# Expert stream of a mixture-of-experts stage: one copy and one split traced elsewhere, rows of empty slots left out of the gather

## The chip, the cores and the metric

One core of a Trainium2 chip runs the whole kernel. The time is device microseconds (us) of one execution; lower is better. The kernel before was run three times, and one more execution was profiled.

## The reference, cut to what matters

The network has two halves. The first (attention and a gated delta rule, two layers) is untouched. The second has two layers, and each ends in a mixture of experts over 512 tokens of width 1024:

```python
def hier_moe(x, ...):                       # 512 tokens, 32 experts, 2 experts a token
    pg_top, g_top = lax.top_k(softmax(xf @ w_rg + b_rg), 1)      # one of 4 groups
    top_p, top_i = lax.top_k(softmax(le_sel), 2)                 # two experts of its 8
    ...
    def expert_block(args):
        idx, e = args
        xb = x_pad[idx]                                          # rows of the tokens routed to e
        hb = jax.nn.silu(xb @ w_gate[e]) * (xb @ w_up[e])        # 1024 -> 512, twice
        return hb @ w_down[e]                                    # 512 -> 1024
```

Every token has two experts, so 1024 (token, expert) pairs are to be computed in each layer. All 32 experts' weights are read in float32: 2 MB each for gate, up and down.

## The kernel before, in words

**Slots.** The kernel gives every expert 64 slots (`BLK`), 2048 in a layer; `route` (L1336) finds for each slot the pair that sits in it, or none. It leaves two integer tables: `tk`, the token of each slot, one column for a pair of experts (L1425 to L1429), and `mp`, the row of the result that each slot is written to (L1430). `tokens` (L1483) makes the first from the matmul result `mps` in two VectorE instructions; an empty slot has 0 there and is given token 0. `slots` (L1489) makes the second, also in two; an empty slot is given an index far above the bound. An expert with more than 64 pairs would be finished in a loop on the device (`For_i`, L1661), whose count is read by every engine.

**Gather.** `rows` (L1496) writes the normalised tokens to a table `xr` in HBM, 512 rows of 4 KB, in four transfers from POOL's queue (L1507). `gather` (L1517) fetches the 128 rows of two experts' slots with one indirect DMA on POOL's queue (L1522) into a tile `xg` of 128x1024, of which there are two in turn. In its second part (after the `yield`) TensorE transposes the tile into two PSUM tiles (L1532), and each half is split into a high part `pk` (ScalarE, L425) and a low part (VectorE, L426; `split`, L412). The last quarter of the second half is also copied whole into `xf` (ScalarE, L1538), after that half's split. Both the split's VectorE part and the copy read the same PSUM tile. Indices over the bound are left out by the indirect DMA (`oob_is_err=False`); the scatter of the results (`finish`, L1616, DMA at L1624) already uses this.

**Expert stream.** `experts` (L1727) walks over units: eight for an expert's gate and up weights, then three for the down weights of the expert before. For the unit six places ahead (`AHEAD`) it cuts the weights into a high and a low part (`cut`, L1565: ScalarE L425, then VectorE L426), then it does the matmuls of the present unit (`inner` L1576, `outer` L1604). Weights come in tiles of 1 MB through SP's queue (L1561), six per expert, into six buffers. `middle` (L1586) stands between gate/up and down: 16 small TensorE products, a tanh on ScalarE (L1596), two VectorE instructions (L1597, L1598), and a split of the result into `hk` (ScalarE L425, VectorE L426). It is traced behind unit (e, 0, 1), and its result is used by the down matmuls behind unit (e, 3, 1). A copy of a finished accumulator to `tmp` (ScalarE, L1765) frees it for the next one.

**Order.** TensorE, VectorE and ScalarE keep the traced order: `pin` (L1627) chains each engine's instructions of the stream. POOL's and SP's instructions are not chained; the scheduler orders them by priority and readiness. Each engine works through its own instructions in order, so one that waits holds up all that stand behind it.

**Before the stream.** `moe` (L1643) routes, gathers the first pair, computes the overflow count (`further`), asks for the first weights and passes the loop, which ran no iteration here. The following pairs are gathered inside `experts`, one for every two experts, 16 in a layer.

Of the kernel before, what the change touches and what calls it, by code (L numbers as in the profile page):

```python
# [13 lines left out]
I32 = mybir.dt.int32  # L14
# [3 lines left out]
OP = mybir.AluOpType  # L18
AX = mybir.AxisListType

P = 128
D = 1024
# [12 lines left out]
N_EXP, D_EXP = 32, 512  # L35
BLK = 64
# [143 lines left out]
class Net:  # L180
# [1155 lines left out]
    def route(self, i):  # L1336

        nc, a = self.nc, self.a
        v, act, pe = nc.vector, nc.scalar, nc.tensor
        X, rstd, gx = self.x_in  # L1340
        ps = self.acc()[:72]
# [11 lines left out]
        table = self.rows(i, gx, rstd)  # L1353
# [36 lines left out]
        for c in range(NC):  # L1390
            o = rk[:, 32 * c:32 * c + 32]
# [3 lines left out]
        for c in range(NC):  # L1395
# [4 lines left out]
                               op0=OP.add, op1=OP.mult)  # L1400
# [16 lines left out]
        mps = self.aux()[:, 0:32]  # L1417
        for k in range(2):
# [3 lines left out]
            for c in range(NC):  # L1422
                pe.matmul(mps, R[:, c].rearrange("p b s -> p (b s)"), idk[:, k, c], start=(k + c == 0),
                          stop=(k == 1 and c == NC - 1))
        tk = self.t([P, N_EXP // 2], "tk", 1, I32)  # L1425
        tk2 = self.t([P, N_EXP], "tk2", 1, I32)
        self.tokens(tk2, mps)
        for b in range(2):
            v.tensor_copy(tk[b * BLK:(b + 1) * BLK], tk2[b * BLK:(b + 1) * BLK, b::2])  # L1429
        mp = self.t([BLK, N_EXP], "mp", 1, I32)  # L1430
        self.slots(mp, mps[:BLK])

        def weights():

# [22 lines left out]
        def further():  # L1457
# [20 lines left out]
            v.tensor_copy(more[:, 0:1], nst[:, 31:32])  # L1478
            v.tensor_scalar(more[:, 1:], bx, float(N_EXP - 1), None, op0=OP.min)
            return place, more  # L1480
        return table, tk, mp, further, weights

    def tokens(self, tk, ps):  # L1483

        v = self.nc.vector
        v.tensor_scalar(tk, ps, -1.0, 0.0, op0=OP.add, op1=OP.max)
        v.tensor_scalar(tk, tk, 1, None, op0=OP.logical_shift_right)

    def slots(self, mp, ps):  # L1489

        v = self.nc.vector
        em = self.t([BLK, N_EXP], "em", 1)[:, :ps.shape[1]]
        v.tensor_scalar(em, ps, 0.0, float(1 << 20), op0=OP.is_equal, op1=OP.mult)
        v.scalar_tensor_tensor(mp, ps, -1.0, em, op0=OP.add, op1=OP.add)

# [18 lines left out]
            self.nc.tensor.transpose(tp[:, j * P:(j + 1) * P], x(j)[:, c * P:(c + 1) * P], self.ident)  # L1514
        return tp

    def gather(self, table, idx, m):  # L1517

        nc = self.nc
        v, act, pe = nc.vector, nc.scalar, nc.tensor  # L1520
        xg = self.t([P, D], "xg", 2)
        nc.gpsimd.indirect_dma_start(out=xg[:m], out_offset=None, in_=table[:, :],  # L1522
                                     in_offset=bass.IndirectOffsetOnAxis(ap=idx, axis=0),
                                     bounds_check=S - 1, oob_is_err=False)
        yield
        n = m // BLK
        pk = self.t([P, KT, n, P], "pk", 2, FR)
        xf = self.t([P, n, BLK], "xf", 2)
        for half in range(2):
            tp = self.aux()  # L1530
            for k in range(4):
                pe.transpose(tp[:, k * m:(k + 1) * m], xg[:m, (4 * half + k) * P:(4 * half + k + 1) * P],  # L1532
                             self.ident[:m, :m])
            tv = tp[:, 0:4 * m].rearrange("p (k e t) -> p k e t", k=4, e=n)
            o = pk[:, 4 * half:4 * half + 4]
            self.split(o[:, :, :, 0:BLK], o[:, :, :, BLK:P], tv)
            if half:
                act.activation(xf, tv[:, 3], AF.Copy)  # L1538
        yield [(pk[:, :, e], xf[:, e]) for e in range(n)]

    def apart(self, ins, first):
# [44 lines left out]
    def middle(self, gu):  # L1586

        nc = self.nc
        v, act, pe = nc.vector, nc.scalar, nc.tensor
        fp = self.aux()  # L1590
        for q in range(2):
            for f in range(4):
                pe.matmul(fp[:, (4 * q + f) * BLK:(4 * q + f + 1) * BLK], gu[q][:, f * P:(f + 1) * P], self.fold,  # L1593
                          start=True, stop=True)
        th = self.t([P, 4 * BLK], "mth", 2)
        act.activation(th, fp[:, 0:256], AF.Tanh, scale=0.5)  # L1596
        v.scalar_tensor_tensor(th, th, 1.0, fp[:, 0:256], op0=OP.add, op1=OP.mult)  # L1597
        v.scalar_tensor_tensor(th, th, 0.5, fp[:, 256:512], op0=OP.mult, op1=OP.mult)  # L1598
        hk = self.t([P, 4, P], "hk", 2, FR)
        hv = th.rearrange("p (f t) -> p f t", f=4)  # L1600
        self.split(hk[:, :, 0:BLK], hk[:, :, BLK:P], hv)
        return hk, hv

    def outer(self, pss, hid, k, h, l, also):  # L1604

# [37 lines left out]
    def moe(self, i, xs, nxt):  # L1643
        nc, a = self.nc, self.a
        v, act, pe = nc.vector, nc.scalar, nc.tensor
        self.compute = [nc.tensor.engine, nc.vector.engine, nc.scalar.engine]
        ym = self.dram.tile([N_SLOT, D], F32, name=f"ym{i}", tag=f"ym{i}", bufs=1)
        table, tk, mp, further, weights = self.route(i)
        pair = lambda q: self.gather(table, tk[:, q:q + 1], P)
        g = pair(0)  # L1650
        next(g)
        place, more = further()

        ws = {}
        for k in range(2):
            ws[0, k] = self.weights(i, 0, k)
        cb = self.t([P, 1], "cb", 1)
        v.memset(cb, 0.0)
        with self.tc.issue_after(self.load.ins):
            extra = nc.values_load(more[0:1, 0:1], min_val=0, max_val=MAX_OVF)  # L1660
        with self.tc.For_i(0, extra, 1) as b:  # L1661
            eo = nc.sync.value_load(more[0:1, bass.ds(b + 1, 1)], min_val=0, max_val=N_EXP - 1)
            sl = self.t([P, BLK], "sl", 1)
            v.tensor_scalar(sl, self.slot1, cb, None, op0=OP.add)
            v.tensor_scalar(cb, cb, float(BLK), None, op0=OP.add)
            bc = lambda x: x.unsqueeze(1).to_broadcast([P, NC, BLK])
            mps = self.aux()[:BLK, 0:1]
            for k in range(2):
                sk = self.t([P, S], "bc", 3).rearrange("p (c s) -> p c s", c=2 * NC)[:, 0:NC]
                v.tensor_tensor(sk, place[:, k * NC:(k + 1) * NC].unsqueeze(2).to_broadcast([P, NC, BLK]), bc(sl),  # L1670
                                op=OP.is_equal)
                for c in range(NC):
                    pe.matmul(mps, sk[:, c], self.ids[:, k * NC + c:k * NC + c + 1], start=(k + c == 0),
                              stop=(k == 1 and c == NC - 1))
            mc, tc = self.t([BLK, 1], "mc", 1, I32), self.t([BLK, 1], "tc", 1, I32)
            self.slots(mc, mps)
            self.tokens(tc, mps)
            go = self.gather(table, tc, BLK)
            next(go)
            self.overflow(i, eo, next(go)[0], mc, ym)  # L1680
        self.tc.no_sync_barrier()
        wt = self.experts(i, ws, [next(g)], pair, mp, ym, weights)
        self.plan((a["w_ple_gate_2"][i], D, 0, D))
        self.fetch(1)
        pp = self.ple_products(i)

        for g in range(2):
            mg = [self.t([P, 2, 2, S], "X", 4) for _ in range(2)]
            for c in range(NC):
                yc = mg[c // 2][:, c % 2]  # L1690
                nc.sync.dma_start(yc, ym.rearrange("(c p k) d -> c p k d", p=P, k=2)[c][:, :, g * S:(g + 1) * S])
                act.activation(yc[:, 0], yc[:, 0], AF.Copy, scale=wt[:, 0, c:c + 1])
                v.scalar_tensor_tensor(yc[:, 0], yc[:, 1], wt[:, 1, c:c + 1], yc[:, 0], op0=OP.mult, op1=OP.add)
            for j in range(4):
                tp = self.transpose4(lambda c: mg[c // 2][:, c % 2, 0, j * P:(j + 1) * P])
                v.tensor_add(xs[4 * g + j], xs[4 * g + j], tp)
                nxt.add(4 * g + j, xs[4 * g + j])
        return pp

    def overflow(self, i, e, x, mp, ym):  # L1700

        room = lambda: self.t([P, S], "bc", 3)
        gu = []
        for up in range(2):
            ps = self.acc()
            for k in range(0, KT, 2):
                w = self.weights(i, e, 2 * up + k // 4, k // 2 % 2)
                m = 1 if k == KT - 2 else 2
# [1 line left out]
                self.inner(ps, x, k, h[:, :m], l[:, :m], w[:, 1] if m == 1 else None)  # L1710
            gu.append(room())
            self.nc.scalar.activation(gu[up], ps, AF.Copy)
        hid = self.middle(gu)
        pss = [self.acc() for _ in range(2)]

        for k in (0, 1):
# [10 lines left out]
    def experts(self, i, ws, xs2, pair, mp, ym, weights):  # L1727
# [3 lines left out]
        nc = self.nc  # L1731
# [8 lines left out]
        acc, gu, hid, g = {}, {}, {}, None  # L1740
        self.pinned = [None, None, {}]
        for n in range(len(units) + AHEAD):
            if n < len(units):
                e, k, part = units[n]
# [3 lines left out]
                m = 1 if k in (1, 3) and part else 2  # L1748
# [6 lines left out]
            e, k, part = units[n - AHEAD]  # L1755
            if k < 4:
# [7 lines left out]
                    gu.setdefault(e, []).append(self.tmp())  # L1764
                    act.activation(gu[e][-1], acc[e], AF.Copy)  # L1765
                if (k, part) == (0, 1) and e:
                    hid[e - 1] = self.middle(gu.pop(e - 1))
                if (k, part) == (2, 1) and e % 2 and e + 1 < N_EXP:
                    xs2.append(next(g))
                if (e, k, part) == (2, 2, 0):  # L1770
# [1 line left out]
            else:  # L1772
                r = k % 2 * 2 + part
                if e == N_EXP - 1 and r == 0:
                    hid[e] = self.middle(gu.pop(e))
                if r == 0:
                    acc[e, "y"] = [self.acc() for _ in range(2)]
                self.outer(acc[e, "y"], hid[e], r, *ready.popleft())
# [179 lines left out]
```

## Time and profile before

| | |
|---|---|
| median of 3 runs | 3080.62 us (3080.24 to 3084.62) |
| profiled execution | 3084.05 us, span 3082.3 us |
| TensorE clock granted over the span | 0.975 |
| busy: TensorE, VectorE, ScalarE, POOL | 93%, 80%, 57%, 15% |
| bytes moved by DMA | 599.29 MB, 248663 packets |
| first expert stream | about 1586 to 2112 us |
| second expert stream | about 2444 to 2968 us |

How to read it: the profile's page gives busy times of the engines over the span, a strip of 40 slices of 77 us, the DMA queues with their bytes, and groups of instructions by line. Other views of the same execution, used below, give busy times and DMA rates of chosen stretches, what each engine waited for, instructions in order of time, and the chain of waits that ended last. Engines: PE is TensorE's matmul, PEld its weight load, DVE VectorE, ACT ScalarE, POOL GpSimd, SPq SyncE's queue. The end of a matmul is modelled, so the start of the next one says more. Shares of busy time are averages over stages with different limits.

### The profile page before, as it was taken

What the parts mean: (1) busy time and instruction counts of PE and PEld (TensorE: products, weight loads), DVE (VectorE), ACT (ScalarE), POOL (GpSimd) and SP (SyncE); (2) the same over time, 40 slices, a digit from 0 to 9 for tenths busy, and PEclk for the clock granted to TensorE, in tenths of its full rate; (3) what the DMA queues carried; (4) which work ended last, traced back from release to release, by engine and by line L of the source; (5) the groups of instructions that cost most, each with busy time, mean ns of one, the idle gap of its engine ahead of it and who ended that gap; (6) DMA issues with size and microseconds to landing.
All of it is one profiled execution on the core that took longest, in us unless ns stands there. A gap on an engine that the chain in (4) does not pass through costs nothing.

```text
span 3082.3 us, 39081 instructions
## 1 busy us (share of the span) xinstructions
PE 2881.6 (93%) x13517; PEld 2160.2 (70%) x13517; DVE 2464.3 (80%) x4540; ACT 1756.1 (57%) x2953; POOL 472.8 (15%) x457
## 2 busy tenths in 40 slices
PE   7998999999999999999979999998998799999987
PEld 6677778886787778878856666665776566666656
DVE  7899787867999578855558888887789588888876
ACT  3454343544454433542357877776476577777874
POOL 1111110011121010120011121111122111121112
PEclk9999999999999999999989999999999899999998
DMA  5211122242222222241259999997123399999981
GB/s 156 82 62 62 62 77 69 83 128 94 74 62 61 77 69 79 86 130 62 95 216 396 406 404 401 407 399 277 65 86 110 151 385 405 404 408 408 406 313 59
DMA packets 248663, 599.29 MB, mean 194 GB/s; under 512 B 29212, under 2 KB 159726, under 8 KB 215694
## 3 DMA queue, kind: packets, MB, share of 16 engines
q1 hardware_dynamic: 237582, 567.38, 49.1%
q0 software_dynamic: 10880, 29.37, 2.7%
q8 instruction: 108, 1.77, 0.2%
q14 instruction: 93, 0.76, 0.1%
HBM read 573.60 MB, written 31.49 MB: 196 GB/s over the span
## 4 chain that ended last, share of the span: by engine, by line
PE 38%; issue 33%; DVE 18%; POOL 7%; ACT 3%; DMA 2%; POOLq 0%; SPq 0%; ACTq 0%; DVEq 0%
PE acc L522 9%; PE acc L521 9%; PE acc L520 9%; POOL ym L1624 4%; DVE wl L426 3%; DVE tmp L953 2%; PE aux L432 1%; POOL xg L1522 1%; PE aux L463 1%; PE aux L843 1%; DMA xg<-xr,tk 1%; PE aux L1111 1%; PE aux L1106 1%; DVE r L1082 1%; DVE r L1081 1%
## 5 line engine op out<-in xcount | busy, mean ns | idle before, releaser
L425 ACT ACTIVATE wh<-w 128x1024 fp32r<-128x1024 f32 (+1 forms) x592 | 577.8, 1003 | 370.2 <-PE acc L521 323.0
L426 DVE TENSOR_TENSOR wl<-w,wh 128x1024 fp32r<-128x1024 f32 (+1 forms) x592 | 674.1, 1164 | 71.1 <-ACT wh L425 66.7
L520 PE MATMUL acc<-X,wh 128*128 128x512 f32 (+1 forms) x1504 | 606.3, 403 | 18.5 <-DVE tmp L898 6.4
L521 PE MATMUL acc<-X,wh 128*128 128x512 f32 (+1 forms) x1536 | 615.8, 401 | 0.6 <-DVE X L426 0.6
L522 PE MATMUL acc<-X,wl 128*128 128x512 f32 (+1 forms) x1504 | 601.9, 401 | 4.9 <-DVE wl L426 4.9
L426 DVE TENSOR_TENSOR X<-w,X 128x1024 fp32r<-128x1024 f32 (+1 forms) x352 | 380.9, 1122 | 64.0 <-ACT X L425 63.2
L425 ACT ACTIVATE X<-w 128x1024 fp32r<-128x1024 f32 (+1 forms) x352 | 326.7, 971 | 34.3 <-DMA w<-in_w_exp_gate_dram 10.1
L520 PEld LDWEIGHTS acc<-X,wh 128*128 128x128 f32 (+1 forms) x1504 | 285.3, 190 | 82.1 <-DVE tmp L898 7.3
L521 PEld LDWEIGHTS acc<-X,wh 128*128 128x128 f32 (+1 forms) x1536 | 291.3, 190 | 59.4 <-DVE X L426 1.2
L522 PEld LDWEIGHTS acc<-X,wl 128*128 128x128 f32 (+1 forms) x1504 | 284.8, 189 | 64.9 <-DVE wl L426 7.1
L1624 POOL DMA_INDIRECT ym<-yb,mp x64 | 136.0, 2125 | 811.9 <-DVE yb L1623 811.9
L1581 PE MATMUL acc<-X,pk 128*128 128x512 f32 x448 | 185.6, 414 | 18.2 <-ACT tmp L1765 12.6
L1581 PE MATMUL acc<-wh,pk 128*128 128x512 f32 x448 | 181.9, 406 | 15.5 <-ACT tmp L1765 15.5
L1584 PE MATMUL acc<-X,pk 128*128 128x512 f32 x448 | 185.9, 415 | 0.0
L1584 PE MATMUL acc<-wl,pk 128*128 128x512 f32 x448 | 183.5, 410 | 0.0
L1583 PE MATMUL acc<-w,xf 128*64 128x512 f32 x256 | 137.3, 618 | 0.0
L1584 PEld LDWEIGHTS acc<-X,pk 128*128 128x128 f32 x448 | 86.3, 193 | 66.0 <-DVE X L426 18.7
L1593 PEld LDWEIGHTS aux<-fold,tmp 128*128 128x128 f32 x1024 | 126.1, 194 | 8.8 <-ACT tmp L1765 3.5
L1584 PEld LDWEIGHTS acc<-wl,pk 128*128 128x128 f32 x448 | 84.5, 189 | 65.8 <-issue 16.2
L479 POOL TENSOR_TENSOR tmp<-tmp,tmp 128x512 f32<-128x512 f32 x60 | 86.4, 1444 | 280.9 <-ACT tmp L472 234.5
L1593 PE MATMUL aux<-fold,tmp 128*128 128x64 f32 x1024 | 123.2, 274 | 3.2 <-ACT tmp L1765 3.2
L1612 PE MATMUL acc<-w,mth 128*64 128x512 f32 x256 | 123.6, 605 | 0.0
(564 smaller groups left out, 5331.8 us busy)
## 6 DMA issues: line engine op xcount, KB each, us to landing
w<-in_w_exp_gate_dram SPq DMA_DIRECT2D x128, 1024.0 KB, 8.0
w<-in_w_exp_up_dram SPq DMA_DIRECT2D x128, 1024.0 KB, 7.8
w<-in_w_exp_down_dram SPq DMA_DIRECT2D x128, 1024.0 KB, 8.4
w<-in_w_in_dram SPq DMA_DIRECT2D x72, 1024.0 KB, 5.1
w<-in_w_in_a_dram SPq DMA_DIRECT2D x12, 1024.0 KB, 5.0
w<-in_w_out_dram SPq DMA_DIRECT2D x8, 1024.0 KB, 5.0
w<-in_w_ple_gate_dram SPq DMA_DIRECT2D x8, 1024.0 KB, 12.1
X<-ym SPq DMA_DIRECT2D x16, 512.0 KB, 5.4
```

Of the source, the lines that this page charges most:

```text
L425: self.nc.scalar.activation(h, x, AF.Copy)
L426: self.nc.vector.tensor_sub(l, x, h.bitcast(F32))
L479: nc.gpsimd.tensor_add(t, tot[0], sq)
L520: mm(ps, wh[:, k], xh[k], start=(k == 0), stop=False)
L521: mm(ps, wh[:, k], xl[k], start=False, stop=False)
L522: mm(ps, wl[:, k], xh[k], start=False, stop=(k == kt - 1))
L1581: pe.matmul(ps, pk[:, k + q], h[:, q], start=(k + q == 0), stop=False)
L1583: pe.matmul(ps[0:BLK], xf, also, start=False, stop=False, skip_group_check=True)
L1584: pe.matmul(ps, pk[:, k + q], l[:, q], start=False, stop=also is not None)
L1593: pe.matmul(fp[:, (4 * q + f) * BLK:(4 * q + f + 1) * BLK], gu[q][:, f * P:(f + 1) * P], self.fold, start=True, stop=True)
L1612: pe.matmul(pss[c][0:BLK], hv[:, 3], also[:, c], start=False, stop=False, skip_group_check=True)
L1624: return nc.gpsimd.indirect_dma_start(out=ym[:, :], out_offset=bass.IndirectOffsetOnAxis(ap=mp, axis=0), in_=y, in_offset=None, bounds_che ...
```

## The change

Three things, and what follows from them:

1. In `gather`, the copy to `xf` is traced ahead of the second half's split and no longer behind it.
2. `middle` becomes a generator of two parts; its last part, the split into `hk`, is traced behind unit (e, 1, 0), one unit later.
3. `slots` now runs on 128 partitions and before `tokens`; the token index is the slot's row shifted right by one. So an empty slot keeps an index far above the bound, and the gather leaves its row out. The two `xg` tiles are made once in a layer and set to zero by POOL ahead of the first gather; a row that is left out keeps what stood there.

```diff
-        tk2 = self.t([P, N_EXP], "tk2", 1, I32)
-        self.tokens(tk2, mps)
+        mp = self.t([P, N_EXP], "mp", 1, I32)
+        tk2 = self.t([P, N_EXP], "tk2", 1, I32)
+        self.slots(mp, mps)
+        self.tokens(tk2, mp)
         for b in range(2):
             v.tensor_copy(tk[b * BLK:(b + 1) * BLK], tk2[b * BLK:(b + 1) * BLK, b::2])
-        mp = self.t([BLK, N_EXP], "mp", 1, I32)
-        self.slots(mp, mps[:BLK])
...
-    def tokens(self, tk, ps):
-        v = self.nc.vector
-        v.tensor_scalar(tk, ps, -1.0, 0.0, op0=OP.add, op1=OP.max)
-        v.tensor_scalar(tk, tk, 1, None, op0=OP.logical_shift_right)
+    def tokens(self, tk, mp):
+        self.nc.vector.tensor_scalar(tk, mp, 1, None, op0=OP.logical_shift_right)
     def slots(self, mp, ps):
-        em = self.t([BLK, N_EXP], "em", 1)[:, :ps.shape[1]]
+        em = self.t([P, N_EXP], "em", 1)[:ps.shape[0], :ps.shape[1]]
         v.tensor_scalar(em, ps, 0.0, float(1 << 20), op0=OP.is_equal, op1=OP.mult)
         v.scalar_tensor_tensor(mp, ps, -1.0, em, op0=OP.add, op1=OP.add)
...
-    def gather(self, table, idx, m):
+    def gather(self, table, idx, m, xg):
-        xg = self.t([P, D], "xg", 2)
...
-            self.split(o[:, :, :, 0:BLK], o[:, :, :, BLK:P], tv)
             if half:
                 act.activation(xf, tv[:, 3], AF.Copy)
+            self.split(o[:, :, :, 0:BLK], o[:, :, :, BLK:P], tv)
...
     def middle(self, gu):
         v.scalar_tensor_tensor(th, th, 0.5, fp[:, 256:512], op0=OP.mult, op1=OP.mult)
+        yield
         hk = self.t([P, 4, P], "hk", 2, FR)
         hv = th.rearrange("p (f t) -> p f t", f=4)
         self.split(hk[:, :, 0:BLK], hk[:, :, BLK:P], hv)
-        return hk, hv
+        yield hk, hv
...
     def moe(self, i, xs, nxt):
         table, tk, mp, further, weights = self.route(i)
-        pair = lambda q: self.gather(table, tk[:, q:q + 1], P)
+        xg = [self.t([P, D], "xg", 2) for _ in range(2)]
+        for x in xg:
+            nc.gpsimd.memset(x, 0.0)
+        pair = lambda q: self.gather(table, tk[:, q:q + 1], P, xg[q % 2])
...
     def experts(self, i, ws, xs2, pair, mp, ym, weights):
                 if (k, part) == (0, 1) and e:
-                    hid[e - 1] = self.middle(gu.pop(e - 1))
+                    mid = self.middle(gu.pop(e - 1))
+                    next(mid)
+                if (k, part) == (1, 0) and e:
+                    hid[e - 1] = next(mid)
...
                 if e == N_EXP - 1 and r == 0:
-                    hid[e] = self.middle(gu.pop(e))
+                    hid[e] = list(self.middle(gu.pop(e)))[1]
```

The overflow loop's body is changed in the same way (its gather uses the second `xg` tile); it ran no iteration.

## Rows read from the trace of the kernel before

**Rows 1.** The page's strip of 40 slices: DMA share, GB/s.

```profile
DMA  5211122242222222241259999997123399999981
GB/s 156 82 62 62 62 77 69 83 128 94 74 62 61 77 69 79 86 130 62 95 216 396 406 404 401 407 399 277 65 86 110 151 385 405 404 408 408 406 313 59
```

**Rows 2.** Busy time by stretch: both streams whole, then the first one's steady part.

```profile
core 0: us, PE busy (x) PEld busy (x) DVE busy (x) ACT busy (x) POOL busy (x), PEclk, DMA share, GB/s
1586.00:2112.00 526.00, 506.95 (x2130) 325.09 (x2130) 463.55 (x547) 413.91 (x586) 87.35 (x45) 0.99 1.00 402
2444.00:2968.00 524.00, 506.13 (x2122) 325.93 (x2120) 460.93 (x545) 411.05 (x583) 84.93 (x45) 0.99 1.00 402
1640.00:2100.00 460.00, 446.93 (x1889) 285.50 (x1888) 407.92 (x475) 364.75 (x516) 79.00 (x40) 1.00 1.00 401
```

**Rows 3.** Who waited for whom, 1640 to 2100: total us, times, longest.

```profile
ACT hk L425 <- DVE mth L1598: 64.1, 28, 2.6
ACT xf L1538 <- DVE pk L426: 23.7, 14, 1.7
ACT X L425 <- DMA w<-in_w_exp_gate_dram: 1.9, 3, 1.0
...
PE acc L1581 <- ACT tmp L1765: 13.1, 15, 1.5
```

**Rows 4.** In order of time, one pair's end: ScalarE, then TensorE.

```profile
1817.61 0.28 ACT L1538 ACTIVATE xf<-aux 128x128 f32<-128x128 f32 x1 [1.71 <-DVE pk L426]
1817.79 1.99 ACT L425 ACTIVATE X<-w 128x1024 fp32r<-128x1024 f32 x2
...
1820.32 0.50 PE L1581 MATMUL acc<-wh,pk 128*128 128x512 f32 x1 [1.45 <-ACT tmp L1765]
```

**Rows 5.** DMA queues over the whole span: packets, MB, share of 16 engines.

```profile
q1 hardware_dynamic: 237582, 567.38, 49.1%
q0 software_dynamic: 10880, 29.37, 2.7%
```

**Rows 6.** POOL's instructions: gather, scatter and table writes (ns min/median/max), a memset (mean ns).

```profile
L1522 POOL DMA_INDIRECT xg<-xr,tk x32: 1008/1149/2011, 1579.0 to 2869.5; - x32
...
L1624 POOL DMA_INDIRECT ym<-yb,mp x64: 896/2236/2261, 1624.9 to 2987.1; - x64
...
L1507 POOL DMA_DIRECT2D xr<-xg x8: 531/540/765, 1567.9 to 2433.2; - x8
...
L1073 POOL MEMSET ty<- 128x512 f32 x16 | 7.9, 524 | 0.0
```

**Rows 7.** Short stretches, columns as in rows 2: rates by stretch, and a fallen clock.

```profile
1600.00:1640.00 40.00, 36.76 (x156) 23.31 (x155) 33.25 (x49) 30.02 (x44) 3.76 (x2) 1.00 1.01 422
...
1646.00:1648.00 2.00, 2.00 (x12) 1.33 (x10) 1.55 (x2) 2.00 (x4) 1.18 (x1) 1.00 0.67 238
...
2500.00:2520.00 20.00, 20.00 (x84) 13.37 (x84) 17.30 (x21) 14.30 (x22) 4.15 (x3) 0.91 0.83 302
```

**Rows 8.** POOL in order of time, first layer's start and two later gathers.

```profile
1575.27 0.53 POOL L1507 DMA_DIRECT2D xr<-xg  x1 [1.28 <-ACT xg L1506]
1579.04 1.08 POOL L1522 DMA_INDIRECT xg<-xr,tk  x1 [3.24 <-DVE rt L1469]
...
1612.16 1.50 POOL L1522 DMA_INDIRECT xg<-xr,tk  x1 [22.88 <-PE aux L1532]
...
1646.82 1.75 POOL L1522 DMA_INDIRECT xg<-xr,tk  x1 [2.40 <-PE aux L1532]
```

**Rows 9.** The first layer's start in order of time: index ready, TensorE goes on.

```profile
1575.82 0.35 DVE L1429 COPY tk<-tk 64x16 int32<-64x16 int32 x2
...
1585.51 1.57 PEld L1532 LDWEIGHTS aux<-ident,xg 128*128 128x128 f32 x8 [10.37 <-issue]
```

**Rows 10.** The chain of waits that ended last, second layer's start.

```profile
2433.17 2.94 DMA xr<-xg
2436.97 4.70 DMA xg<-xr,tk
```

More of the change, by code (lines that the diff above doesn't have):

```diff
@@ L1480, in further @@
             return place, more
-        return table, tk, mp, further, weights
-    def tokens(self, tk, ps):
-        v = self.nc.vector
-        v.tensor_scalar(tk, ps, -1.0, 0.0, op0=OP.add, op1=OP.max)
-        v.tensor_scalar(tk, tk, 1, None, op0=OP.logical_shift_right)
+        return table, tk, mp[:BLK], further, weights
+    def tokens(self, tk, mp):
+        self.nc.vector.tensor_scalar(tk, mp, 1, None, op0=OP.logical_shift_right)
     def slots(self, mp, ps):
         v = self.nc.vector
-        em = self.t([BLK, N_EXP], "em", 1)[:, :ps.shape[1]]
+        em = self.t([P, N_EXP], "em", 1)[:ps.shape[0], :ps.shape[1]]
         v.tensor_scalar(em, ps, 0.0, float(1 << 20), op0=OP.is_equal, op1=OP.mult)
@@ L1676, in moe @@
             self.slots(mc, mps)
-            self.tokens(tc, mps)
-            go = self.gather(table, tc, BLK)
+            self.tokens(tc, mc)
+            go = self.gather(table, tc, BLK, xg[1])
             next(go)
@@ L1712, in overflow @@
             self.nc.scalar.activation(gu[up], ps, AF.Copy)
-        hid = self.middle(gu)
+        hid = list(self.middle(gu))[1]
         pss = [self.acc() for _ in range(2)]
```

## The prediction, made before the changed kernel was run

> **What bounds the kernel now.** I start with the strip of the page [rows 1]: DMA stands at 9 tenths or more and moves about 400 GB/s in two blocks of slices only, and they are the two expert streams. All three edits act there or just ahead of it, so I look at nothing else. The busy times by stretch [rows 2] show 526 and 524 us, 1050 us in all; in both the DMA share is 1.00 at 402 GB/s, TensorE is busy for 96 to 97% of the time and VectorE for 88%. Two things could thus set the pace, and I take them one after the other.
>
> The waits [rows 3] show the engines' side. In 460 us ScalarE hardly waits for weights (one such wait of 1.9 us stands there as an example), but 64.1 us for VectorE ahead of `hk` and 23.7 us ahead of `xf`. What this costs TensorE is seen once in a pair of experts [rows 4]: the copy to `xf` waits 1.71 us for VectorE's part of the split, the cuts behind it start late, and behind those stands the accumulator copy (L1765) for which TensorE then waits 1.45 us. The sum of those waits of TensorE is 13.1 us in 460 [rows 3].
>
> The DMA side: at a share of 1.00 over 1050 us [rows 2] no engine of the sixteen has room to spare, and SP asks for a tile as soon as a buffer is free. So I take DMA as the bound, and the engines as second, close behind it: 13.1 us of 460 is 2.8% of the time, and that much the engines could go faster if DMA let them.
>
> TensorE's 96% [rows 2] would leave no room at all. In the same row its weight loads are busy for 325.09 of 526 us, 62%. The Trainium skill (Perfetto Trace Analysis, Identifying the Most-Contended Engine) says that matmul occupancy is no good measure of how near TensorE is to its limit, and that weight-load occupancy is one. By that rule TensorE has room and the whole DMA saving shows; by the 96% nearly none would. Nothing below rests on this paragraph: the cap used is the 13.1 us.
>
> **Part 1: rows left out.** How many rows are empty can be read from the queues. POOL's queue, q0, moved 29.37 MB [rows 5]. The 32 gathers of 128 rows of 4 KB are 16.78 MB and the 8 table writes of 512 KB are 4.19 MB [rows 6]. 8.40 MB are left for 64 scatters, which are 2050 rows: the 2 times 1024 pairs, and not the 2 times 2048 slots. So rows that a scatter leaves out move no bytes, and half the slots are empty (32 gathers also say that no overflow iteration ran). The gathers will move half of 16.78 MB. One gather in 16 goes ahead of the stream, so 15/16 of 8.39 MB, 7.86 MB, leave the saturated stretches. At 402 GB/s [rows 2] that is 19.6 us; by the price of q1 (49.1% of 3082.3 us for 567.38 MB, 2.67 us per MB [rows 5]) 21.0; by that of q0 (2.7% for 29.37 MB, 2.83 us per MB) 22.3. I take **-19.6**, the rate of the very stretch.
>
> The rate is not even: 422 GB/s from 1600 to 1640, but 238 from 1646 to 1648 [rows 7], next to the gather issued at 1646.82 [rows 8]. Were the whole stream at 422, 1050 us would shrink by 4.7%, 50 us. No row says what makes the dips. Against the gathers' rows as cause: the gather of 1612.16 [rows 8] lies inside the stretch at 422, and the dip at 1646 is there before that gather's rows can move. Bounds 0 and -50; if the half of the dips that lies behind a gather's issue came from its rows, halving these would give a quarter of 50, 12.5. I take a third of that, **-4**, because of the gather without a dip.
>
> **Part 2: the new start.** The index is one VectorE instruction later, 0.1 to 0.2 us. It is ready at 1576.2 [rows 9], the gather goes out at 1579.04 [rows 8]: nothing, 2.8 us of cover. What the gather waits for is the table's last write (issued at 1575.27, 0.53 us long, then 3.24 us of idle POOL [rows 8]; its landing in the second layer, 2.94 us, is on the chain [rows 10]). VectorE has one instruction less there in all: nothing. The two memsets are new on POOL's queue ahead of the first gather. A 128x512 one took 524 ns [rows 6]; one of 128x1024 I estimate by its size at 1.05 us. The first zeroes the tile of the third table write and is done while the fourth is on its way. The second may start only when that fourth write has read its tile, which is about when the gather could go. So it is on the path: **+1.05** per layer; bounds 0 (the scheduler puts it behind the gather) and 2.1.
>
> Everything waits for that first gather: it takes 4.70 us to land [rows 10], and TensorE goes on at 1585.51 behind 10.37 us of idle [rows 9], since the loop lets no engine pass before. With half the rows it lands sooner; bounds are 4.70 and the 2.94 us of a table write [rows 10], which also brings 128 rows of 4 KB. I take 4.0, **-0.7** per layer. POOL's own time for it could rise to what a scatter with rows left out takes, 2236 ns instead of 1149 [rows 6]: 0 to +1.1. Later gathers have POOL's idle time as cover (busy 79.00 of 460 us [rows 2]), and their landing has half a pair to spare. For both layers the start costs **+0.7** us, between -3.5 and +6.4.
>
> **Part 3: `xf` and `hk`.** No instruction is added. `xf` ahead of the split no longer waits for VectorE; the split behind it is 0.28 us later [rows 4], and its result has the next units as cover. `hk` is split one unit later; in between ScalarE cuts the next weights, about 1 us, in place of waiting up to 2.6 us [rows 3]. Behind the moved instruction stand only cuts six units ahead of their use, and the down matmuls need `hk` six units later: nothing is queued that anyone waits for. If all of TensorE's 13.1 us go [rows 3], the engines' side gets shorter by 13.1/460 of 1050 us, 30 us; if the wait only moves to the new place of `hk`, by nothing. This and part 1 do not add: the later of the two sides sets the time. 23.6 is less than 30, so DMA sets it and part 3 is the leave to collect part 1.
>
> Sum: -19.6 - 4 + 0.7 = -22.9 us. The profiled execution took 3084.05 us (span 3082.3), 3.4 above the median of 3080.62. From the median this gives **3058 us**.
>
> **Rivals.** (a) The sixteen DMA engines save unevenly. Filled slots are the first of each expert's 64, so an engine that serves those keeps its rows, and a tile of weights has landed only when the last engine is done. The saving is then between 0 and 19.6; half of it, 9.8, with no gain in the dips and +0.7 gives 3072. For it: the share of 1.00 is a mean of sixteen. Against: several tiles are in flight, so an engine may lag for a while. The Trainium skill (DMA: Bandwidth & Descriptors, The descriptor swizzle) ties each engine to fixed partitions of a 128-partition transfer, which is what this rival needs; no row here shows engines apart.
>
> (b) The gathers make the dips, and both sides get free: -30 by the engines' cap gives 3051. The ends of matmuls are modelled and may hide part of a wait, so I let the range go 10 us further. For: the place of the dip. Against: the gather of 1612.16.
>
> (c) No change: the wait for VectorE only moves one unit on, TensorE's 13.1 us stay, and the engines keep the pace while DMA gets idle time; or rows left out cost a gather as much as rows moved. 3081. For: ScalarE's few waits for weights [rows 3]. Against: the share of 1.00, and the scatters' bytes.
>
> (d) Slower: the clock. Where TensorE had waited, its granted clock was 0.91 in one stretch of 20 us, between its levels of 1.2 and 2.4 GHz, and the rate fell to 302 GB/s [rows 7], 5 us lost by 402. If a stream that waits for DMA in place of ScalarE gives TensorE longer gaps, this could come back in each stream; from five such stretches on it eats the 23 us, at seven (35 us) the result is 3093. Against: in the steady 460 us the clock was 1.00 [rows 2], and fewer bytes mean fewer gaps.
>
> **How the numbers follow.** Chances: forecast 0.50, (a) 0.14, (b) 0.22, (c) 0.10, (d) 0.04. The predicted time is the forecast's, 3058. The range reaches to (a) at 3072 and 10 us past (b), to 3041; (c), (d) and what lies beyond either end are left out, about 2 in 10. What a measurement here can tell from no change is 0.2%, 6.2 us: forecast, (a) and (b) are faster by more, 0.86; (c) is the same, 0.10; (d) slower, 0.04.
>
> **What would show it.** Right: q0's bytes fall by 8.4 MB to about 21.0; both streams get some 11 us shorter at an unchanged DMA share of 1.00 and 402 to 408 GB/s; ScalarE's wait at `xf` is gone, that at `hk` smaller, and waits for weights take their place; the first gather goes out about 1 us later behind its table write. Wrong: a DMA share well below 1.00 in the streams (then the engines set the pace, and part 3 is worth what was gained), a rate that rises towards 422 (b), a wait of TensorE for ScalarE that is as long as before (c), or a granted clock below 1.00 inside a stream (d).

## The result and the profile after

The changed kernel takes 3040.99 us (median of 4 runs, 3040.12 to 3042.76), the kernel before beside it 3082.62: a ratio of 0.9864, 95% interval 0.9849 to 0.9879, or 41.6 us faster. The forecast was 22.9 us faster. The time lies at the very edge of the range, 0.01 us under its low end of 3041. The direction held, the size forecast was little more than half of what came, and the reason given for it was the wrong one, as the experiments show.

The steady part of the streams, by stretch (columns as in [rows 2]):

```profile
1640.00:2080.00 440.00, 439.80 (x1874) 284.01 (x1874) 402.94 (x471) 365.99 (x511) 76.54 (x40) 1.00 1.01 410
2500.00:2900.00 400.00, 400.00 (x1708) 258.76 (x1706) 366.76 (x428) 335.17 (x468) 69.93 (x36) 1.00 1.01 412
```

TensorE is busy for 439.80 of 440 us; before it was 446.93 of 460 [rows 2], 97%. The DMA share is what it was, 1.01 for 1.00, yet the rate went up from 401 to 410 GB/s. The same share now goes with another rate.

Who waited for whom in 1640 to 2080 (total us, times, longest):

```profile
ACT hk L425 <- DVE mth L1595: 28.1, 27, 1.4
...
ACT X L425 <- DMA w<-in_w_exp_gate_dram: 11.6, 15, 1.9
ACT wh L425 <- DMA w<-in_w_exp_gate_dram: 10.8, 9, 3.0
...
ACT wh L425 <- DMA w<-in_w_exp_up_dram: 9.0, 13, 1.1
...
ACT X L425 <- DMA w<-in_w_exp_up_dram: 7.1, 14, 1.0
...
PEld acc L1578 <- ACT tmp L1766: 2.0, 5, 0.5
```

The kernel before in the same stretch, cut to what answers:

```profile
ACT hk L425 <- DVE mth L1598: 61.8, 27, 2.6
...
ACT xf L1538 <- DVE pk L426: 22.2, 13, 1.7
...
PE acc L1581 <- ACT tmp L1765: 12.1, 14, 1.5
```

These are the waits of [rows 3], there for a longer stretch. Now the wait ahead of `xf` is gone, that ahead of `hk` has more than halved, TensorE's waits for the accumulator copy are gone but for 2.0 us of its weight loads. ScalarE waits for weights in their place, 43.8 us in all, where before it was 5.8. It got ahead of the data, where before it was behind.

ScalarE in order of time, at the place of [rows 4], and the start of TensorE's next accumulation:

```profile
1649.16 0.27 ACT L1534 ACTIVATE xf<-aux 128x128 f32<-128x128 f32 x1
...
1649.79 2.01 ACT L425 ACTIVATE X<-w 128x1024 fp32r<-128x1024 f32 x2
1651.69 0.61 ACT L1766 ACTIVATE tmp<-acc 128x512 f32<-128x512 f32 x1
...
1653.13 0.19 PEld L1578 LDWEIGHTS acc<-X,pk 128*128 128x128 f32 x1
```

No bracket stands behind the copy to `xf` any more, and the accumulator copy is done at 1652.30, before TensorE starts on an accumulator again.

POOL's DMA queue on the page, and the new start of the first layer (POOL in order of time):

```profile
q0 software_dynamic: 10880, 20.99, 1.9%
```

```profile
1578.72 0.53 POOL L1505 DMA_DIRECT2D xr<-xg  x1 [1.27 <-ACT xg L1504]
1579.92 0.95 POOL L1649 MEMSET xg<- 128x1024 f32 x1 [0.67 <-DMA xr<-xg]
1581.72 0.95 POOL L1649 MEMSET xg<- 128x1024 f32 x1 [0.85 <-DMA xr<-xg]
1582.84 1.08 POOL L1519 DMA_INDIRECT xg<-xr,tk  x1 [0.17 <-POOL xg L1649]
```

The bytes are as counted: 29.37 MB before [rows 5], 20.99 now, 8.38 less. The gather goes out 4.12 us behind the issue of the last table write, before 3.77 [rows 8]: the memsets cost 0.35 us and not 1.05. The chain has the first gathers' landings:

```profile
1582.84 4.14 DMA xg<-xr,tk
...
2417.27 3.45 DMA xg<-xr,tk
```

In the second layer it was 4.70 [rows 10].

All of the gain lies in the streams. From the first gather's issue to the last scatter's they took 551.6 and 550.1 us before, and take 529.7 and 528.5: 43.5 us less, more than the 41.6 of the whole.

### The profile page after: what moved, and what is told of

Its sections match the earlier page's. It is cut to its first block, busy times and chain, and to the rows that moved or that the text cites. A ratio compares the mean times of both kernels' runs of the same rounds, so it can differ in the third digit from the quotient of the medians.

```text
span 3040.7 us, 39079 instructions
## 1 busy us (share of the span) xinstructions
PE 2879.0 (95%) x13517; PEld 2164.6 (71%) x13517; DVE 2461.4 (81%) x4538; ACT 1766.8 (58%) x2953; POOL 473.8 (16%) x461
## 2 busy tenths in 40 slices
DMA packets 248663, 590.91 MB, mean 194 GB/s; under 512 B 31260, under 2 KB 161774, under 8 KB 215694
## 3 DMA queue, kind: packets, MB, share of 16 engines
q0 software_dynamic: 10880, 20.99, 1.9%
## 4 chain that ended last, share of the span: by engine, by line
PE 40%; issue 32%; DVE 17%; POOL 7%; ACT 3%; DMA 2%; POOLq 0%; SPq 0%; ACTq 0%; DVEq 0%
PE acc L522 10%; PE acc L521 10%; PE acc L520 10%; POOL ym L1622 4%; DVE wl L426 2%; DVE tmp L953 2%; PE aux L432 2%; POOL xg L1519 1%; PE aux L463 1%; PE aux L843 1%; PE aux L1111 1%; PE aux L1106 1%; DMA xg<-xr,tk 1%; DVE r L1081 1%; PE aux L828 1%
## 5 line engine op out<-in xcount | busy, mean ns | idle before, releaser
L425 ACT ACTIVATE wh<-w 128x1024 fp32r<-128x1024 f32 (+1 forms) x592 | 584.9, 1006 | 415.3 <-PE acc L521 327.9
L425 ACT ACTIVATE X<-w 128x1024 fp32r<-128x1024 f32 (+1 forms) x352 | 333.5, 976 | 69.6 <-DMA w<-in_w_exp_gate_dram 30.3
```

Of the source, the lines that this page charges most:

```text
L425: self.nc.scalar.activation(h, x, AF.Copy)
```

## The experiments

A measure that serves for all of them is the time of a pair of experts: from the third scatter of a stream to the 29th there are 13 pairs. The scatters' starts in the first stream, from POOL in order of time; the changed kernel first:

```profile
1658.59 2.24 POOL L1622 DMA_INDIRECT ym<-yb,mp  x1 [10.60 <-DVE yb L1621]
...
2073.91 1.63 POOL L1622 DMA_INDIRECT ym<-yb,mp  x1 [13.73 <-DVE yb L1621]
```

The kernel before:

```profile
1660.40 2.24 POOL L1624 DMA_INDIRECT ym<-yb,mp  x1 [11.84 <-DVE yb L1623]
...
2090.38 2.23 POOL L1624 DMA_INDIRECT ym<-yb,mp  x1 [15.73 <-DVE yb L1623]
```

| kernel | us a pair, first stream | second stream | GB/s, 1640 to 2080 | ratio to before, 95% interval |
|---|---|---|---|---|
| before | 33.08 | 33.08 | 401 | 1 |
| rows_only | 32.76 | 32.77 | 397 | 0.9966 (0.9951 to 0.9982) |
| hk_only | 32.12 | 32.28 | 413 | 0.9930 (0.9911 to 0.9949) |
| xf_only | 31.88 | 32.31 | 416 | 0.9914 (0.9892 to 0.9935) |
| order_only | 31.91 | 31.97 | 417 | 0.9894 (0.9875 to 0.9913) |
| changed | 31.95 | 31.84 | 410 | 0.9864 (0.9849 to 0.9879) |
| no_rows | 31.89 | 32.12 | 404 | 0.9883 (0.9866 to 0.9899) |
| more_pe | 32.75 | 32.76 | 401 | 0.9971 (0.9961 to 0.9981) |
| cut_more | 31.34 | 31.57 | 416 | 0.9845 (0.9828 to 0.9861) |

### The change in its parts

**rows_only**: the changed kernel with copy and split back in their old places.

```diff
+            self.split(o[:, :, :, 0:BLK], o[:, :, :, BLK:P], tv)
             if half:
                 act.activation(xf, tv[:, 3], AF.Copy)
-            self.split(o[:, :, :, 0:BLK], o[:, :, :, BLK:P], tv)
...
-                    mid = self.middle(gu.pop(e - 1))
-                    next(mid)
-                if (k, part) == (1, 0) and e:
-                    hid[e - 1] = next(mid)
+                    hid[e - 1] = self.middle(gu.pop(e - 1))
```

> Only the rows of empty slots are left out (with the two memsets); copy and split stand where they stood before. Theory A (each part relieves its own side, and the later of the two sides sets the pace): the engines' waits are as before, TensorE still waits about 13 us in 460 for ScalarE, so the rows alone give little, 3 to 12 us, and DMA's share falls below 1.00. Theory B (DMA alone is the bound): the rows give most of the 41 us, 30 or more. Theory C (two gains that add): about 20 us.

Measured: 0.9966, about 10 us. The steady part and its waits:

```profile
1640.00:2080.00 440.00, 432.44 (x1834) 278.32 (x1834) 393.57 (x459) 350.82 (x496) 73.96 (x39) 1.00 1.00 397
...
PE acc L1578 <- ACT tmp L1765: 7.6, 12, 1.5
```

With fewer bytes the rate fell to 397 GB/s at a share of 1.00. So the share does not say that DMA is full. Theory B is refuted; A's size is met, though the share stayed at 1.00 where A had it fall. TensorE's wait also went down, from 12.1 us in the same stretch of the kernel before to 7.6; how fewer bytes help ScalarE there is not shown by any run.

**order_only, xf_only, hk_only**: the kernel before with both moves, with the copy alone and with the split alone.

```diff
+            if half:
+                act.activation(xf, tv[:, 3], AF.Copy)
             self.split(o[:, :, :, 0:BLK], o[:, :, :, BLK:P], tv)
-            if half:
-                act.activation(xf, tv[:, 3], AF.Copy)
...
```

The split is moved as the change moves it.

> Only the copy to xf and the split to hk are traced elsewhere; empty slots still fetch token 0. Theory A: DMA moves as many bytes as before at a share of 1.00, so the gain is what the rate can still give, 5 to 20 us, and ScalarE waits for weights. Theory B: nothing, within 3 us, at 402 GB/s. Theory C: about 20 us, at about 410 GB/s.

> Only the copy to xf is traced ahead of the split. If TensorE's wait of 1.45 us a pair comes from the copy's wait of 1.71 us, it is gone here and this kernel takes nearly all of what both moves give. If the wait for VectorE ahead of hk feeds it as well, it takes less than half.

> Only the split to hk is traced one unit later. If TensorE's wait for ScalarE comes from the copy to xf, it stays at about 13 us in 460 here and the time is within 5 us of the kernel before. If it comes from ScalarE's waits ahead of hk, it is gone and the gain is that of both moves.

Measured: 0.9894 for both, 33 us; 0.9914 for the copy, 26 us; 0.9930 for the split, 22 us. The moves alone bring most of the gain with every byte still moved, at 417 GB/s. All theories put it too low, A's 5 to 20 us too. The single moves, of which one was to bring nearly all and the other little, lie between: 8 and 7 tenths of the 33 us. The steady part of order_only, and the waits of hk_only in 1640 to 2080:

```profile
1640.00:2080.00 440.00, 439.93 (x1883) 285.02 (x1882) 404.76 (x473) 369.39 (x513) 76.57 (x40) 1.00 1.01 417
```

```profile
ACT hk L425 <- DVE mth L1598: 29.9, 27, 1.4
...
ACT xf L1538 <- DVE pk L426: 23.3, 14, 1.7
...
PE acc L1581 <- ACT tmp L1766: 2.2, 5, 0.7
```

In hk_only the wait ahead of `xf` is as long as before, and still TensorE's wait has nearly gone. So the 1.45 us that [rows 4] show behind the copy to `xf` were not that copy's alone. The reading that fits both runs is that ScalarE was late by the sum of its waits in a pair, and that either move takes most of that away. For the same reason 26 and 22 do not add to 48: at 31.9 us a pair TensorE has no more waiting to lose. The copy alone gets there in the first stream (31.88) but not in the second (32.31 for order_only's 31.97).

### What sets the pace now

**more_pe**: the changed kernel with two of `middle`'s eight small products done twice.

```diff
+        for f in range(2):
+            pe.matmul(fp[:, (4 + f) * BLK:(5 + f) * BLK], gu[1][:, f * P:(f + 1) * P], self.fold, start=True, stop=True)
         th = self.t([P, 4 * BLK], "mth", 2)
```

> The changed kernel with two of middle's eight small TensorE products done a second time for every expert (same result). In the changed kernel 16 instructions of the eight products take 1.70 us from the first start to the next group's, so two more are 0.43 us an expert, 27 us in 64 experts. Theory A (TensorE now sets the pace of the streams, gapless): slower than the changed kernel by 20 to 30 us. Theory B (DMA sets it): slower by less than 8 us.

Measured: 3071.64 us, beside 3040.98 of no_memset (below) on the same chip: 31 us slower, by theory A's 20 to 30 us and slightly more. A pair takes 0.80 us more (32.75 for 31.95), about what four added products of TensorE make (0.86). DMA gave way, and the waits for weights stayed:

```profile
1640.00:2080.00 440.00, 440.00 (x1929) 288.86 (x1928) 395.28 (x458) 359.16 (x500) 70.27 (x39) 1.00 1.00 401
...
ACT wh L425 <- DMA w<-in_w_exp_gate_dram: 16.8, 19, 1.9
...
ACT X L425 <- DMA w<-in_w_exp_gate_dram: 12.9, 13, 1.9
...
SPq L1558 <- PE acc L1580: 191.8, 54, 4.7
SPq L1558 <- PE acc L1612: 105.4, 27, 4.2
```

A share of 1.00 again, at 401 GB/s, with TensorE setting the pace. ScalarE waits 45.4 us in all for weights here, while DMA moves no more than in the kernel before, where ScalarE waited 5.8. So such waits do not by themselves mean that DMA is the bound. SP's queue, which asks for the weights, waits 297 us of the 440 for TensorE to finish with a tile: by this road the pace of TensorE becomes the rate of DMA.

**no_rows**: the changed kernel, whose gathers in the streams move nothing (`none` is a column of indices above the bound).

```diff
+        if q:
+            idx = self.none
         nc.gpsimd.indirect_dma_start(out=xg[:m], out_offset=None, in_=table[:, :],
```

> The changed kernel, but after the first pair of each layer every index lies above the bound, so the gathers in the streams move no row: the tokens of the other 30 experts aren't fetched, and the expert products use what stood in the tiles. Theory A (TensorE sets the pace): within 6 us of the changed kernel, DMA at about 402 GB/s. Theory B (DMA sets it): another 7.9 MB are saved, so 19 us faster than the changed kernel, at 410 GB/s or more.

Measured: 3045.21 us, 0.9883: no faster than the changed kernel (4 us behind no_memset on the same chip), and 31.89 us a pair at 404 GB/s. The first stream is the one to compare, since the second layer routes by what the first one left. Once copy and split are moved, the bytes of the gathers are worth nothing in the steady part. more_pe and no_rows together show that TensorE sets the pace of the changed streams.

**cut_more**: the changed kernel, with one more quarter of an expert's weights cut in two parts, so that TensorE is spared one of its slow float32 products.

```diff
-                m = 1 if k in (1, 3) and part else 2
+                m = 1 if k == 1 and part else 2
...
-            pe.matmul(ps, pk[:, k + q], l[:, q], start=False, stop=also is not None)
+            pe.matmul(ps, pk[:, k + q], l[:, q], start=False, stop=also is not None or k + q == KT - 1)
```

> The changed kernel, but of the two quarters per expert's gate and up weights that are multiplied uncut (in two slow float32 instructions), the one of the up weights is cut in two parts like the others. TensorE then needs 1.32 - 0.23 - 0.46 = 0.63 us less per expert, ScalarE and VectorE about 0.6 us more. Theory A (TensorE sets the pace): faster than the changed kernel by 10 to 25 us, until DMA at up to 420 GB/s holds it. Theory B (DMA sets it): within 4 us of the changed kernel, or slower, since VectorE has more to do.

**no_memset** and **cut_more2**: the first writes the table from two fixed tiles, which the gathers then use, so nothing has to be zeroed; the second adds cut_more's edit to it.

```diff
+        tiles = [self.t([P, D], "xg", 2) for _ in range(2)]
+        self.row_tiles = tiles
         for c in range(NC):
-            o = self.t([P, D], "xg", 2)
+            o = tiles[c % 2]
...
-        xg = [self.t([P, D], "xg", 2) for _ in range(2)]
-        for x in xg:
-            nc.gpsimd.memset(x, 0.0)
+        xg = self.row_tiles
```

> The changed kernel without the two memsets: the gathers use the two tiles that held the last rows of the table, so rows that are left out keep those. If the second memset delays the first gather by its 0.95 us, the start of each stream is 1 us earlier and the time 2 us less than the changed kernel's; if the table's write lands only then, less than 0.7 us.

> The changed kernel once more, beside the two below on the same chip. Theory A and theory B alike: 0.986 to 0.987 of the kernel before.

> The changed kernel without the memsets and with the second uncut quarter cut like the others. Theory A (TensorE sets the pace): as the kernel with that cut alone, 8 to 12 us faster than the changed kernel; the missing memsets add less than 1 us. If the cut's gain was a chance of that chip, within 4 us of the changed kernel.

Measured: no_memset 3040.98 us, ratio 0.9871 (0.9855 to 0.9888), no different from the changed kernel: the memsets cost nothing that shows in the time. In the trace the gather goes out 3.77 and 3.79 us behind the last table write, for 4.12 and 4.15 with the memsets: 0.35 us a layer, which is the second of the two cases. cut_more 3030.49 us, 10.5 less than no_memset on the same chip, the low end of theory A. On another chip the changed kernel took 3045.65 us, ratio 0.9877 (0.9860 to 0.9894), a little above the 0.986 to 0.987 expected, and cut_more2 3031.49, ratio 0.9836 (0.9820 to 0.9852): 14 us less, theory A and a little more than its 8 to 12. The two kernels with that cut are the fastest found and can't be told apart. The forecast for the cut was 0.63 us an expert, 1.26 a pair; 0.61 came in the first stream and 0.27 in the second. The first stream of cut_more, and what TensorE waited for:

```profile
1640.00:2080.00 440.00, 435.73 (x1911) 294.52 (x1911) 422.95 (x479) 381.80 (x520) 92.36 (x41) 1.00 1.01 416
...
PE acc L1578 <- ACT tmp L1766: 2.4, 7, 0.6
...
PE acc L1607 <- DVE hk L426: 1.8, 6, 0.4
```

VectorE is busy for 96% (92% in the changed kernel), TensorE has gaps again: 4.3 us of 440, or 0.3 us a pair, nearly all of them these two waits. TensorE's busy time a pair fell by 0.90 us, by these shares, and not by 1.26. So nearly half of what is missing is the gaps, and the rest is that the cut saved TensorE less than was worked out for it.

### Bytes or one row read over and over

**before_spread**: the kernel before, with different tokens in the empty slots (`spare` grows by 8 from partition to partition).

```diff
+        f = self.t([P, N_EXP], "tkf", 1)[:ps.shape[0], :ps.shape[1]]
+        v.tensor_scalar(f, ps, 0.0, None, op0=OP.is_equal)
+        v.scalar_tensor_tensor(f, f, self.spare[:ps.shape[0]], ps, op0=OP.mult, op1=OP.add)
-        v.tensor_scalar(tk, ps, -1.0, 0.0, op0=OP.add, op1=OP.max)
+        v.tensor_scalar(tk, f, -1.0, 0.0, op0=OP.add, op1=OP.max)
```

> The kernel before, but empty slots fetch different tokens (by their partition) and no longer all token 0; two VectorE instructions more per layer ahead of the first gather. As many bytes move as before. If the rows left out paid for being one row read over and over, this kernel has that gain too, 8 to 12 us. If they paid as bytes and descriptors, it is within 4 us of the kernel before.

Measured: 1.0006 (0.9996 to 1.0017). That empty slots all read token 0 cost nothing that shows. What is left as the source of rows_only's 10 us is that fewer rows move.

## Why the prediction was wrong

**The bound.** The step that failed is "So I take DMA as the bound, and the engines as second". It rested on a share of 1.00. The runs show that share at 397, 401, 404, 410 and 417 GB/s: it does not say that no more would fit. In its place the runs show the engines as the bound: in the kernel before, ScalarE's order held TensorE up (order_only gave 33 us and took DMA to 417 GB/s with every byte still moved); in the changed kernel TensorE itself sets the pace (0.80 us a pair more for 0.86 us more work, and nothing for 7.9 MB less). The rows of the kernel before had the hint: ScalarE hardly ever waited for weights (the row in [rows 3], three waits and not one, is 1.9 us of 460). The Trainium skill (Perfetto Trace Analysis, Identifying the Most-Contended Engine) says of DMA that occupancy misleads, since there are sixteen engines, and wants the throughput against the peak in its place. These runs agree about the occupancy, with 397 to 417 GB/s at one share; the throughput did not tell the bound either, at 401 GB/s both in the kernel before and in more_pe.

Most of what the prediction put down as signs of being right came true: q0's bytes, a share of 1.00, the waits at `xf` and `hk`, the waits for weights. All of these come as well when TensorE is the bound, so they could not tell the two apart; the streams, shorter by 22 us each and not by 11, and the rate of 410 beyond 408 could.

**Part 3** was put down as "the leave to collect part 1", with no gain of its own. It stood in the sum at nothing, and alone it is worth 33 us; its cap, 30 us by TensorE's 13.1 us of waits in 460, was nearly its size. TensorE's waits were the right rows; they were only placed second.

**Part 1**: the bytes were right (8.38 MB for 8.39), their price was not. -19.6 us stood for them; alone they gave 10, and on top of the moves 5 to 9 (0.9877 or 0.9864 for 0.9894, intervals that overlap). By the traces most of the second figure is won at the streams' starts: from the first gather's issue to the third scatter's, order_only takes 77.1 and 76.9 us, the changed kernel 75.8 and 73.1, while their pairs take about as long afterwards (31.91 and 31.97, 31.95 and 31.84). That "this and part 1 do not add" is thus true of the steady part only, where the later side does set the time; but the side was TensorE's, not DMA's.

**The dips**, -4: not the gathers' rows. Of the 220 pieces of 2 us between 1640 and 2080, 16 are below 350 GB/s in the kernel before, 18 in rows_only, with half the rows, and 2 in order_only, with all of them. So the moves took the dips away and the rows did not, which fits places where the engines were late.

**The start**: +1.05 for the memset was 0.35. The second memset, 0.95 us long, starts 3.00 us behind the issue of the last table write, and without memsets the gather goes out at 3.77 (no_memset): most of the memset lies ahead of the time at which the gather could go. -0.7 for the landing was 0.69 in the first layer (4.14 for 4.83) and 1.25 in the second. The sum, +0.7 for both layers, came out as a gain of 1.2 us.

**Hidden costs**: that `hk` and `xf` delay nobody held in the changed kernel; in cut_more, where TensorE has less to do, it waits 1.8 us in 440 for `hk`. The index, one VectorE instruction later, held as well: the gather waits for the second memset and not for the index.

**Rivals.** (b) gave the nearest time by the wrong road: its -30 is the engines' cap, which was the right term, but the dips were not the gathers'. That the time came within 0.01 us of the range, whose low end was (b) and 10 us more for waits hidden in modelled matmul ends, is luck; run again, the same kernel took 3045.65 us (after_again). (a) has lost its ground, since DMA did not set the pace; no run shows the sixteen engines apart. (c) had the engines keeping the pace, and by the right row; it went wrong over the moves: the wait ahead of `hk` did not just move on but fell from 61.8 to 28.1 us in the same stretch, and TensorE's wait went away. (d): the clock stayed at 1.00 in both steady stretches. The paragraph on TensorE's room needs a correction too: by the rule that it quotes, weight loads busy for 62% mean room, but at 284.01 of 440 us, 65%, TensorE was the bound (more_pe). As a sign of whether TensorE has time to spare, the Trainium skill's measure misleads here, and the measurement decides. What keeps the share of the weight loads low while TensorE is never idle was not tried apart.

## What to carry to other kernels

A DMA share of 1.00 is no proof of a DMA bound: look whether the engine that takes the data in waits for it. If it hardly does, and waits for another engine, the bound is not DMA. The reverse does not hold: in more_pe ScalarE waited 45.4 us for weights, and TensorE was the bound. In an order fixed by hand, put a step that must wait for a busy engine behind the next independent work, and a copy that needs no one ahead of the step that does: a wait of 2 us on ScalarE, twice or three times in 33, cost TensorE 1.1 us a pair. Before pricing the saving of one resource, add a known amount of work to the other and see whether it shows: more_pe and no_rows told it for the changed kernel in one run each. On the kernel before, neither was tried.

## What the runs showed of the hardware

The DMA share of a stretch stayed at 1.00 to 1.01 while its rate went from 397 to 417 GB/s, with the pace of the engines and the bytes of a pair. Rows left out of an indirect gather move no data, but the count of q0's packets did not change: 10880 before and after, 29.37 and 20.99 MB, and the page's count under 512 B rose from 29212 to 31260, by 2048, one small packet for every row left out. A memset of 128x1024 float32 on POOL took 0.95 us. Reading one 4 KB row of HBM over and over cost nothing that shows against reading different rows (1.0006).
